# Attention and recurrence of a hybrid trunk layer: each store issued by the engine that makes its data

## The chip, the cores and the metric

The kernel runs on one core of a Trainium2 chip. The metric is the time of one execution on the device in microseconds (us); of several runs the median is given. The core has TensorE (PE in the profile, with its weight loads as PEld), VectorE (DVE), ScalarE (ACT), GpSimd (POOL) and SyncE (SP). Each works through its own instructions in order. A DMA is issued by an instruction in the queue of one engine, and an engine whose next instruction has to wait holds back everything behind it.

## The reference, cut to what matters

One layer of a hybrid backbone on 1024 latent tokens and 256 prompt tokens, 1024 channels, in float32. The normalised input is projected to everything that the two mixers need. Attention has 8 heads of 64 on 2 key/value heads; latent tokens read 512 cached and 1024 latent keys, prompt tokens read the 256 prompt keys. The recurrence (HGRN) has 4 heads of 128 and runs forwards and backwards in chunks of 32.

```python
z = h @ w_in
hq, hf_f, hf_b, hi, hg, aq, ak, av, gl = jnp.split(z, _split_points(), axis=-1)
...
s = jnp.einsum('bqkgd,bskd->bkgqs', qi, kf) * scale
p = jax.nn.softmax(s, axis=-1)
return jnp.einsum('bkgqs,bskd->bqkgd', p, vf)
...
def step(s, inp):
    dec, kv_n = inp
    return dec[..., None] * s + kv_n, s
...
merged = g[:, :, 0] * (o_h @ w_ho) + g[:, :, 1] * (o_a @ w_ao)
return merged @ w_out, k, v, s_final
```

Behind it come a gated residual, a second norm, a squared-ReLU MLP and the last norm. Outputs are both token sets, the prompt's new keys and values, and the final states of the recurrence.

## The kernel before, in words

All products are made in three passes of split operands (a rounded high part and the rest). The order of TensorE's instructions is the order in which the program is written (L50); the instructions of the other engines are put in order by a scheduler from its own estimate of when each can run, SyncE's DMA issues among them, up to the MLP (from L1332 SyncE's order is the written one too). Tiles come from rings of a few buffers (L31 to L43): a tile is written again only when the readers of its former content are done. Query loads, key loads, scratch of the recurrence and the exponentials' high parts share ring X with 20 buffers; weight loads (`wraw`, L293) have two buffers, their split forms (`wsp`, L298) six.

**Attention** (`attention`, L804) is made of 20 units: 16 of one head by 512 latent queries with 12 key blocks of 128, and 4 of two heads by 256 prompt queries with 2 key blocks. Keys lie on the partitions, so a score tile is 128 keys by 512 queries. A unit does this:
- `load_q` (L691) loads its queries from scratch in DRAM as Ql (Qp for the prompt), `load_q2` (L695) once more as Q2, whose row 64 is kept for the maxima.
- `top` (L700) makes a first score (L708) whose maximum over the keys (L709) is wanted for each query. `top_row` (L713) turns the four columns of maxima into rows (`mrow`) and four small DMAs, one for each block of 128 queries, put them into row 64 of Q2, so that the next product subtracts them.
- `score` (L722) makes the score tile of one key block (L726) in one of two PSUM banks; ScalarE takes the exponential in place in PSUM (L728) and copies its rounded high part out as pTh (L730), VectorE makes the rest, pTl (L731), GpSimd adds up pTh (pacc, L735).
- `value` (L738) multiplies with the values (L745, L746); `sums` (L753) adds the row sums (L755); `scale` (L766) divides on GpSimd (oa, L771) and stores the result to DRAM (OA).

These steps of neighbouring units overlap by a table of due times in units of one score step (L815 to L833): the queries of a unit are loaded 15 steps before its first score and first used 1.9 steps later; the row of maxima of the unit before it is due 0.4 steps ahead of that load; the result of the unit before that is stored 6 steps after its last score.

Between the steps of attention TensorE works on the **projections for the recurrence** (`Filler`, L364): `z_ch` (L343) makes channels by tokens, `z_tok` (L323) tokens by channels. Each result is taken out of PSUM by a function `..._consume` and stored to DRAM: queries QD by ScalarE alone (`hq_consume`, L849), forget gates FD by ScalarE and then VectorE (`hf_consume`, L857), values VD by ScalarE (`hi_consume`, L867), output gates GD by ScalarE, VectorE and then GpSimd (`hg_consume`, L874). All these evacuation tiles (`ze`) come from one ring of four.

The **recurrence** (`hgrn`, L1043) has 24 units (head, direction, token tile). Each loads uf, uq, uv and, backwards, ug from that scratch (`prep`, L895), runs scans on VectorE, and is filled up on TensorE with the projection of the branch gates (`gl_consume`, L1086, stored as GT). The transposed result is taken out by ScalarE and stored as OH (`out_t`, L1034); the final states come from VectorE and are stored to the output (L1067).

In the kernel before all of these stores are issued by SyncE with the helper `dma` (L106), in the same queue as the loads of queries, keys, values, scratch and weights. The helper `store` (L109), which issues from GpSimd's queue, serves the small rows of sums, the gate rows, and the MLP.

Of the kernel before, what the change touches and what calls it, by code (L numbers as in the profile page):

```python
# [15 lines left out]
P = 128  # L16
# [29 lines left out]
def build(ctx, tc, I, O, C):  # L46
    nc = tc.nc
    v, s_, g_, pe, sp = nc.vector, nc.scalar, nc.gpsimd, nc.tensor, nc.sync
# [8 lines left out]
    def pool(name, side="left"):  # L57

        st = open_pools[name] = ExitStack()
        return st.enter_context(tc.tile_pool(name=name, bufs=1, side=side, reuse_waits="tile"))  # L60
# [16 lines left out]
    def PS(tag, shape=(P, 512)):  # L77
        if tag in turn and not rings_of_two:
            turn[tag] += 1
            tag = third[tag] if turn[tag] % 3 == 0 else tag  # L80
        return ps.tile(list(shape), F32, tag=tag, name="ps_" + tag, bufs=PSB[tag])

    def S(shape=(P, 512), dt=F32, name=None, ring=None):
        ring = ring or RING_OF[name]
        return (xb if ring == "X" else sb if ring in "DE" else sl).tile(list(shape), dt, tag="s" + ring, name=name, bufs=RINGS[ring])

    def res(store, t, kc, name):

        if t < 2:
            store[t][kc] = S(name=name)  # L90
        elif kc % 2 == 0:
            x = S((P, 2, 256), name=name)
            store[t][kc], store[t][kc + 1] = x[:, 0, :], x[:, 1, :]
        return store[t][kc]
# [8 lines left out]
    def DR(shape, name, dt=F32):  # L103
        return dp.tile(list(shape), dt, name=name)

    def dma(out, in_):  # L106
        sp.dma_start(out=f32(out), in_=f32(in_))

    def store(out, in_):  # L109
        g_.dma_start(out=f32(out), in_=f32(in_))  # L110

    def f32(ap):
        return ap.bitcast(F32)
# [486 lines left out]
    for idx in range(len(steps)):  # L600
        while idx >= KC - 1 and done <= min(idx + AHEAD, len(steps) - 1):
            t, kc = steps[done]
# [7 lines left out]
        t, kc = steps[idx]  # L610
# [59 lines left out]
    OH = [[DR((P, n), "OH%d_%d" % (c, t)) for t, (_, n, _) in enumerate(TT)] for c in range(4)]  # L670

    class Unit:
# [40 lines left out]
        def top_row(self):  # L713

            pt = PS("t")
            pe.transpose(pt[0:4, 0:P], self.ngm, ident)
            r = S((4, P), F32R, name="mrow")
            s_.activation(r, pt[0:4, 0:P], AF.Copy)
            for b in range(4):
                dma(self.q2[64:65, b * P:(b + 1) * P], r[b:b + 1, :])  # L720

        def score(self, k):  # L722
            kg, b = self.kt[k]
# [29 lines left out]
        def sums(self):  # L753

            pe.matmul(self.pl, sel1[0], self.acc, start=False, stop=True, skip_group_check=True)  # L755
            r = S(name="prow")
            with tc.high_priority(offset=400):
                s_.activation(r[64:65], self.pl[64:65], AF.Copy)
                v.tensor_tensor(self.o, self.pl[0:64], self.o, op=ALU.add)
            row, inv, rs = SR[self.h][self.t], RR[self.h][self.t], T(4, "rs")  # L760
            store(row, r[64:65])
            g_.dma_start(out=rs, in_=row.rearrange("o (p j) -> (o p) j", j=4))
            v.reciprocal(rs, rs)
            store(inv.rearrange("o (p j) -> (o p) j", j=4), rs)

        def scale(self):  # L766

            row = RR[self.h][self.t]
            o, rb = self.o, S((64, 512), name="prb")
            g_.dma_start(out=rb, in_=row.broadcast_to([64, 512]))  # L770
            g_.tensor_tensor(o, o, rb, op=ALU.mult)  # L771
            oa = OA[self.h // 2][self.t]
            if self.t < 2:
                d0 = (self.h % 2) * 64
                dma(oa[d0:d0 + 64, :], o)
            else:
                dma(oa.rearrange("(h d) n -> d h n", h=2), self.view(o))

    SR = [[DR((1, 512), "SR%d_%d" % (h, t)) for t in range(3)] for h in range(8)]
    RR = [[DR((1, 512), "RR%d_%d" % (h, t)) for t in range(3)] for h in range(8)]  # L780
# [63 lines left out]
    QD = [[DR((P, n), "QD%d_%d" % (h, t)) for t, (_, n, _) in enumerate(TT)] for h in range(4)]  # L844
    FD = [[[DR((P, n), "FD%d_%d_%d" % (d, h, t)) for t, (_, n, _) in enumerate(TT)] for h in range(4)] for d in range(2)]
    VD = [[DR((P, NB[t], 256), "VD%d_%d" % (c, t)) for t in range(3)] for c in range(2)]
    GD = [[DR((P, NB[t], 256), "GD%d_%d" % (c, t)) for t in range(3)] for c in range(2)]

    def hq_consume(c):  # L849
        def f(half, t, po):  # L850
            n = TT[t][1]
            e = S(name="ze")
            s_.activation(e[:, 0:n], po, AF.Copy, scale=float(P) ** -0.5)
            dma(QD[2 * c + half][t], e[:, 0:n])
        return f

    def hf_consume(d, c):  # L857
        def f(half, t, po):
            n = TT[t][1]
            h = 2 * c + half  # L860
            e = S(name="ze")
            s_.activation(e[:, 0:n], po, AF.Tanh, scale=0.5)
            v.tensor_scalar(e[:, 0:n], e[:, 0:n], fc1[:, d, h:h + 1], fc0[:, d, h:h + 1], op0=ALU.mult, op1=ALU.add)
            dma(FD[d][h][t], e[:, 0:n])
        return f

    def hi_consume(c):  # L867
        def f(pr, po):
            e = S((P, 2, 256), name="ze")
            s_.activation(e, po, AF.Copy)  # L870
            dma(VD[c][pr // 2][:, 2 * (pr % 2):2 * (pr % 2) + 2], e)
        return f

    def hg_consume(c):  # L874
        def f(pr, po):
            e = S((P, 4, P), name="ze")
            po4 = po.rearrange("p b (h d) -> p (b h) d", h=2)
            s_.activation(e, po4, AF.Tanh, scale=0.5)
            v.scalar_tensor_tensor(e.rearrange("p a d -> p (a d)"), e.rearrange("p a d -> p (a d)"), 1.0,
                                   po.rearrange("p b d -> p (b d)"), op0=ALU.add, op1=ALU.mult)  # L880
            g_.tensor_tensor(e, e, hnb.unsqueeze(1).broadcast_to([P, 4, P]), op=ALU.mult)
            dma(GD[c][pr // 2][:, 2 * (pr % 2):2 * (pr % 2) + 2], e.rearrange("p (b h) d -> p b (h d)", b=2))
        return f


    class HUnit:
# [147 lines left out]
        def out_t(self):  # L1034
            nb = self.nb
            pt = PS("t", (P, 4, P))
            for b in range(nb):
                pe.transpose(pt[:, b, :], self.o[:, b], ident)
            e = S((P, 4, P), name="oT")
            s_.activation(e[:, 0:nb], pt[:, 0:nb], AF.Copy)  # L1040
            dma(OH[self.h][self.t], e[:, 0:nb].rearrange("p b d -> p (b d)"))

    def hgrn(fill):  # L1043

        units = hunits
        fwd = {u.h: {} for u in units}
        for u in units:
            u.fwd = fwd[u.h].get(u.t)
            fwd[u.h][u.t] = u
        N, LATE = len(units), 3  # L1050

        share = [u.n + 128.0 for u in units] + [300.0] * LATE
        tot, done, st = sum(share), 0.0, None
        units[0].keys_t()
        for i in range(N + LATE):
            part = lambda x: fill.to((done + x * share[i]) / tot)
            if i + 1 < N:
                units[i + 1].prep()
            if i < N:
                u = units[i]  # L1060
                part(0.25)
                u.scores(u.fwd)
                part(0.5)
                u.states_(u.st or st)
                st = u.last
                if u.t == 2:
                    dma(O["new_state_hgrn"][u.d, u.h], st)  # L1067
                part(0.75)
            if i >= LATE and units[i - LATE].d == 1:
                units[i - LATE].out_t()  # L1070
            if 1 <= i <= N:
                units[i - 1].out(units[i - 1].fwd)
            part(0.95)
            if i + 1 < N:
                units[i + 1].keys_t()
            if 1 <= i <= N and units[i - 1].d == 1:
                units[i - 1].gate(units[i + 1] if i + 1 < N else None)
            part(1.0)
            done += share[i]


    GT = [[DR((P, n), "GT%d_%d" % (c, t)) for t, (_, n, _) in enumerate(TT)] for c in range(16)]

    def gl_consume(c):
        def f(half, t, po):
            n = TT[t][1]  # L1086
            e = S(name="ze")
            s_.activation(e[:, 0:n], po, AF.Tanh, scale=0.5)
            dma(GT[2 * c + half][t], e[:, 0:n])
        return f  # L1090

    def zh(c):
# [65 lines left out]
    for t in MT:  # L1158
        n = TT[t][1]
        for c in range(8):  # L1160
            r = S(name="or")
# [18 lines left out]
    for c2 in range(4):  # L1180
        r = wp.tile([P, 8, 256], F32, tag="wraw", name="wraw", bufs=2)
        for i, nm in enumerate(("w_hgrn_out", "w_attn_out")):
            dma(r[:, 4 * i:4 * i + 4, :], I[nm][:, c2 * 256:(c2 + 1) * 256].rearrange("(k p) c -> p k c", p=P))
        for half in range(2):
# [4 lines left out]
            for t in MT:  # L1189
                n = TT[t][1]  # L1190
# [108 lines left out]
    for b, half in turns:  # L1299
        t, off = b // 4, (b % 4) * P  # L1300
# [62 lines left out]
    def raw1(i):  # L1363
        return wraw(I["w_ff1"], KC, i * 256)
# [30 lines left out]
    for i in range(NP):  # L1395
        r = raw1(i)
        for half in range(2):
# [6 lines left out]
            if half == 0:  # L1404

                x = pw.tile([P, 4, P], F32, tag="at", name="at", bufs=4)
                e = pw.tile([P, 4, P], F32, tag="ap", name="ap", bufs=3)
# [124 lines left out]
    st = pool("st")  # L1532
# [291 lines left out]
```

## Time and profile before

| | |
|---|---|
| median of 3 runs | 2151.84 us (2149.25 to 2152.53) |
| the profiled execution | 2148.34 us |
| its span in the profile | 2146.6 us |
| mean granted clock of TensorE | 0.983 of full speed |
| VectorE busy | 1358.9 us (63%) |
| ScalarE busy | 967.0 us (45%) |
| GpSimd busy | 670.4 us (31%) |
| DMA: queue of SyncE (hardware) | 281.92 MB, 41.0% of 16 engines' span |
| DMA: queue of GpSimd (software) | 42.41 MB, 5.8% |

All times in the profile are counted from the start of the span, in us unless marked ns. A line of the waits reads: engine, what it was about to make, its line, `<-` whom it waited for, then the total, how many times, and the longest. A line of the timeline reads: start, duration, engine, line, operation, out`<-`in, count, and in brackets the idle time just before it with what ended it. SPq is SyncE's queue of DMA issues; since every such issue goes through one helper, they all have its line, L107, and are told apart by tile names. The time of a DMA issue is the time it takes on the issuing engine; the time to landing is the transfer's own. In names of tiles the buffer numbers are left out, so Q2 stands as `Q`. Attention runs from about 190 to 790 us, the recurrence from there to about 1090, the output projection to about 1300, then the MLP.

### The profile page before, as it was taken

What the parts mean: (1) busy time and instruction counts of PE and PEld (TensorE: products, weight loads), DVE (VectorE), ACT (ScalarE), POOL (GpSimd) and SP (SyncE); (2) the same over time, 40 slices, a digit from 0 to 9 for tenths busy, and PEclk for the clock granted to TensorE, in tenths of its full rate; (3) what the DMA queues carried; (4) which work ended last, traced back from release to release, by engine and by line L of the source; (5) the groups of instructions that cost most, each with busy time, mean ns of one, the idle gap of its engine ahead of it and who ended that gap; (6) DMA issues with size and microseconds to landing.
All of it is one profiled execution on the core that took longest, in us unless ns stands there. A gap on an engine that the chain in (4) does not pass through costs nothing.

```text
span 2146.6 us, 31802 instructions
## 1 busy us (share of the span) xinstructions
PE 2025.3 (94%) x11296; PEld 1697.0 (79%) x11296; DVE 1358.9 (63%) x2405; ACT 967.0 (45%) x1812; POOL 670.4 (31%) x757
## 2 busy tenths in 40 slices
PE   6899988988989978999999999999999999999997
PEld 4698767876767867888888888998888888888886
DVE  4785654555655556987644644866666666667785
ACT  4764655555555622222240323764454544333442
POOL 1461455564545654655402200121222210000010
PEclk9999999999999988999999999999999999999999
DMA  9365223133222233554564442584444459545773
GB/s 298 124 202 158 64 82 89 42 107 106 73 79 69 77 123 114 160 169 133 179 198 135 136 157 106 185 260 146 157 143 157 160 213 373 190 146 177 229 255 112
DMA packets 242496, 326.36 MB, mean 152 GB/s; under 512 B 27640, under 2 KB 158800, under 8 KB 242336
## 3 DMA queue, kind: packets, MB, share of 16 engines
q1 hardware_dynamic: 227040, 281.92, 41.0%
q0 software_dynamic: 15296, 42.41, 5.8%
q8 instruction: 89, 1.46, 0.3%
q14 instruction: 71, 0.58, 0.1%
HBM read 236.55 MB, written 87.65 MB: 151 GB/s over the span
## 4 chain that ended last, share of the span: by engine, by line
PE 56%; DVE 4%; DMA 2%; ACT 1%; issue 1%; POOL 0%; SPq 0%; DVEq 0%; POOLq 0%; ACTq 0%
PE ps_g L319 3%; PE ps_g L321 3%; PE ps_g L320 3%; PE ps_v L319 2%; PE ps_g L1627 1%; PE ps_v L321 1%; PE ps_v L320 1%; PE ps_g L1625 1%; PE ps_g L1626 1%; PE ps_t L1625 1%; PE ps_t L1626 1%; PE ps_t L1627 1%; PE ps_s L1475 1%; PE ps_t L1473 1%; PE ps_t L1474 1%; PE ps_t L1475 1%
## 5 line engine op out<-in xcount | busy, mean ns | idle before, releaser
L319 PE MATMUL ps_g<-hs,wsp 128*128 128x512 f32 (+1 forms) x688 | 250.4, 364 | 0.0
L735 POOL TENSOR_TENSOR pacc<-pacc,pTh 128x512 f32<-128x512 f32 x160 | 208.4, 1303 | 117.8 <-ACT pTh L730 102.8
L321 PE MATMUL ps_g<-hs,wsp 128*128 128x512 f32 (+1 forms) x688 | 241.7, 351 | 1.4 <-DVE wsp L291 1.4
L320 PE MATMUL ps_g<-hs,wsp 128*128 128x512 f32 (+1 forms) x688 | 241.8, 352 | 0.0
L290 ACT ACTIVATE wsp<-wraw 128x1024 fp32r<-128x1024 f32 x110 | 109.7, 998 | 264.6 <-PE ps_g L320 73.7
L291 DVE TENSOR_TENSOR wsp<-wraw,wsp 128x1024 fp32r<-128x1024 f32 x110 | 135.4, 1232 | 138.5 <-ACT wsp L290 138.2
L731 DVE TENSOR_TENSOR pTl<-ps_s,pTh 128x512 fp32r<-128x512 f32 x200 | 137.3, 687 | 114.0 <-ACT pTh L730 97.4
L728 ACT ACTIVATE ps_s<-ps_s 128x512 f32<-128x512 f32 x200 | 116.6, 583 | 198.5 <-PE ps_s L726 180.2
L709 DVE TENSOR_REDUCE mx<-ps_t 128x1 f32<-128x512 f32 (+1 forms) x208 | 136.7, 665 | 83.8 <-PE ps_t L708 82.9
L290 ACT ACTIVATE ah<-ar 128x640 fp32r<-128x640 f32 (+1 forms) x112 | 81.0, 723 | 190.7 <-PE ps_v L1626 102.3
L319 PEld LDWEIGHTS ps_g<-hs,wsp 128*128 128x128 f32 x688 | 131.8, 192 | 23.7 <-issue 5.0
L321 PEld LDWEIGHTS ps_g<-hs,wsp 128*128 128x128 f32 x688 | 131.3, 191 | 19.6 <-DVE wsp L291 1.6
L320 PEld LDWEIGHTS ps_g<-hs,wsp 128*128 128x128 f32 x688 | 132.0, 192 | 17.6 <-issue 0.2
L291 DVE TENSOR_TENSOR ah<-ar,ah 128x640 fp32r<-128x640 f32 (+1 forms) x112 | 89.8, 802 | 80.3 <-ACT ah L290 79.9
L708 PE MATMUL ps_t<-Kl,Ql 128*128 128x512 f32 x192 | 85.0, 443 | 46.7 <-DMA Ql<-QS 38.2
L730 ACT ACTIVATE pTh<-ps_s 128x512 fp32r<-128x512 f32 x200 | 119.4, 598 | 13.5 <-ACT ps_s L728 0.4
L172 POOL TENSOR_TENSOR frst<-ms,mexp 128x1 f32<-128x1 f32 x10 | 11.4, 1152 | 362.7 <-DVE ssf L1714 278.4
L336 PE MATMUL ps_g<-wsp,hs 128*128 128x256 f32 x400 | 117.6, 294 | 0.0
L338 PE MATMUL ps_g<-wsp,hs 128*128 128x256 f32 x400 | 114.5, 286 | 0.0
L337 PE MATMUL ps_g<-wsp,hs 128*128 128x256 f32 x400 | 114.4, 286 | 0.0
L708 PEld LDWEIGHTS ps_t<-Kl,Ql 128*128 128x128 f32 x192 | 37.1, 193 | 63.2 <-DMA Ql<-QS 42.5
L336 PEld LDWEIGHTS ps_g<-wsp,hs 128*128 128x128 f32 x400 | 77.7, 194 | 10.4 <-issue 2.4
(562 smaller groups left out, 5914.7 us busy)
## 6 DMA issues: line engine op xcount, KB each, us to landing
ar<-AF SPq DMA_DIRECT2D x112, 320.0 KB, 3.3
wraw<-in_w_ff SPq DMA_DIRECT2D x32, 1024.0 KB, 5.8
wr<-in_w_ff SPq DMA_DIRECT2D x128, 256.0 KB, 4.3
wraw<-in_w_in SPq DMA_DIRECT2D x18, 1024.0 KB, 6.3
wraw<-in_w_ada SPq DMA_DIRECT2D x16, 1024.0 KB, 6.0
AF<-a POOLq DMA_DIRECT2D x48, 256.0 KB, 2.7
AF<-t POOLq DMA_DIRECT2D x48, 256.0 KB, 2.5
wa<-in_w_ada SPq DMA_DIRECT2D x32, 256.0 KB, 5.9
```

What stands on the lines that cost most here:

```text
L290: s_.activation(hi, raw, AF.Copy)
L291: v.tensor_tensor(lo, raw, f32(hi), op=ALU.subtract)
L319: pe.matmul(out, hi[:, k, :], mh, start=(first and k == 0), stop=False)
L320: pe.matmul(out, hi[:, k, :], ml, start=False, stop=False)
L321: pe.matmul(out, lo[:, k, :], mh, start=False, stop=(last and k == kcs - 1))
L336: pe.matmul(po[:, bb, :], mh[:, off:off + P], wh[:, k % 4, :], start=(k == 0), stop=False)
L708: pe.matmul(pq[:, 0:n], self.q1[:, b * P:(b + 1) * P], K[self.g][0][self.kts[i]], start=True, stop=True)
L709: v.tensor_reduce(self.mx[:, i:i + 1], pq[:, 0:n], axis=AX.X, op=ALU.max)
L728: s_.activation(pq, pq, AF.Exp)
L730: s_.activation(hi, pq, AF.Copy)
L731: v.tensor_tensor(lo, pq, f32(hi), op=ALU.subtract)
L735: g_.tensor_tensor(self.acc, f32(self.pt[0][0]) if k == 1 else self.acc, f32(hi), op=ALU.add)
```

## The change

A helper `store_act` issues a DMA from ScalarE's queue. Ten stores in nine functions leave SyncE (the one of OA in two forms). To ScalarE go those whose data ScalarE makes: the row of maxima (80 issues), QD (12), VD (10), OH (12) and GT (48). To GpSimd, by the helper `store`, go OA (20 issues) and GD (10), whose data GpSimd makes, and FD (24) and the final states (8), whose data VectorE makes, which issues no DMA. What is stored, from where and to where, and all tiles, rings and due times are the same. The loads all stay on SyncE; so do the stores of the stage before attention (keys, queries and values to scratch).

```diff
     def store(out, in_):
         g_.dma_start(out=f32(out), in_=f32(in_))
+
+    def store_act(out, in_):
+
+        s_.dma_start(out=f32(out), in_=f32(in_))
...
             r = S((4, P), F32R, name="mrow")
             s_.activation(r, pt[0:4, 0:P], AF.Copy)
             for b in range(4):
-                dma(self.q2[64:65, b * P:(b + 1) * P], r[b:b + 1, :])
+                store_act(self.q2[64:65, b * P:(b + 1) * P], r[b:b + 1, :])
...
             if self.t < 2:
                 d0 = (self.h % 2) * 64
-                dma(oa[d0:d0 + 64, :], o)
+                store(oa[d0:d0 + 64, :], o)
             else:
-                dma(oa.rearrange("(h d) n -> d h n", h=2), self.view(o))
+                store(oa.rearrange("(h d) n -> d h n", h=2), self.view(o))
...
-            dma(QD[2 * c + half][t], e[:, 0:n])
+            store_act(QD[2 * c + half][t], e[:, 0:n])
...
-            dma(FD[d][h][t], e[:, 0:n])
+            store(FD[d][h][t], e[:, 0:n])
...
-            dma(VD[c][pr // 2][:, 2 * (pr % 2):2 * (pr % 2) + 2], e)
+            store_act(VD[c][pr // 2][:, 2 * (pr % 2):2 * (pr % 2) + 2], e)
...
-            dma(GD[c][pr // 2][:, 2 * (pr % 2):2 * (pr % 2) + 2], e.rearrange("p (b h) d -> p b (h d)", b=2))
+            store(GD[c][pr // 2][:, 2 * (pr % 2):2 * (pr % 2) + 2], e.rearrange("p (b h) d -> p b (h d)", b=2))
...
-            dma(OH[self.h][self.t], e[:, 0:nb].rearrange("p b d -> p (b d)"))
+            store_act(OH[self.h][self.t], e[:, 0:nb].rearrange("p b d -> p (b d)"))
...
                 if u.t == 2:
-                    dma(O["new_state_hgrn"][u.d, u.h], st)
+                    store(O["new_state_hgrn"][u.d, u.h], st)
...
-            dma(GT[2 * c + half][t], e[:, 0:n])
+            store_act(GT[2 * c + half][t], e[:, 0:n])
```

## The prediction

> **What bounds the kernel now.** I read the page first, then the waits of TensorE, then the waits of SyncE's DMA queue, then the two engines' timelines side by side where TensorE stands still.
>
> ```profile
> span 2146.6 us, 31802 instructions
> PE 2025.3 (94%) x11296; PEld 1697.0 (79%) x11296; DVE 1358.9 (63%) x2405; ACT 967.0 (45%) x1812; POOL 670.4 (31%) x757
> ```
>
> The span is 2146.6 us; TensorE is busy for 2025.3 of it. What can be won is in the 121 us in which TensorE is idle, and in stretches in which it works at a lower clock. The windows say where the edited stages stand:
>
> ```profile
> 190.00:490.00 300.00, 268.38 (x1438) 221.81 (x1438) 171.10 (x304) 162.25 (x289) 153.50 (x140) 0.96 0.28 84
> 490.00:790.00 300.00, 270.86 (x1502) 222.71 (x1502) 173.59 (x299) 162.60 (x290) 166.07 (x156) 0.97 0.26 76
> 850.00:1090.00 240.00, 237.79 (x1870) 200.71 (x1870) 179.82 (x422) 67.20 (x183) 115.41 (x132) 0.99 0.52 162
> ```
>
> The columns are the stretch and its length, then the busy time of TensorE, its weight loads, VectorE, ScalarE and GpSimd, then the granted clock. In attention (190 to 790) TensorE is idle for 31.6 + 29.1 = 60.7 us; in the recurrence (850 to 1090) for 2.2. So attention decides. Who makes TensorE wait there:
>
> ```profile
> PE ps_t L708 <- DMA Ql<-QS: 38.2, 13, 5.6
> PE ps_t L966 <- DVE usf L937: 16.9, 2, 14.8
> PE ps_t L708 <- DVE mx L709: 8.5, 11, 1.3
> PE ps_t L708 <- DMA Qp<-QS: 7.6, 4, 3.7
> PE ps_s L726 <- DVE pTl L731: 6.8, 2, 6.1
> ```
>
> Three quarters of attention's idle time, 38.2 + 7.6 = 45.8 us in 17 gaps, is the first product with a freshly loaded query block (Ql, or Qp for the prompt) waiting for that load. The load is short once it is issued:
>
> ```profile
> DMA to landing us min/median/max: 3.2/3.5/8.2
> ```
>
> So why is it issued late? Around the gap that ends at 299.27, SyncE's queue and then TensorE:
>
> ```profile
> 284.21 8.04 SPq L107 DMA_DIRECT2D OA<-oa  x2
> 292.34 2.45 SPq L107 DMA_DIRECT2D Q<-mrow  x4
> 294.89 0.53 SPq L107 DMA_DIRECT2D FD<-ze  x1
> 295.52 0.38 SPq L107 DMA_DIRECT2D Ql<-QS  x1
> ```
> ```profile
> 299.27 0.80 PE L708 MATMUL ps_t<-Kl,Ql 128*128 128x512 f32 x1 [5.12 <-DMA Ql<-QS]
> ```
>
> TensorE wanted Ql at 299.27 - 5.12 = 294.15. SyncE works its queue in order, and from 284.21 to 295.52 it had nothing but stores: two OA stores (the second waited for GpSimd), four issues for the row of maxima, one FD store. Over the whole kernel these waits are
>
> ```profile
> SPq L107 <- DVE wsp L291: 354.1, 38, 27.0
> ...
> SPq L107 <- POOL oa L771: 105.8, 18, 13.4
> SPq L107 <- DVE ze L863: 92.1, 13, 17.0
> ```
>
> The top row is no store: weight loads (wraw) wait there for their buffer. The bound, then, is TensorE, and in attention a load behind stores in one queue.
>
> **The change, part by part.** The sum is made against the profiled execution, 2148.34 us (span 2146.6 and 1.7 around it). The median shown is 2151.84, 3.5 more; I add that at the end.
>
> *The query loads.* All stores ahead of Ql and Qp (mrow to ScalarE, OA, FD and GD to GpSimd, VD and QD to ScalarE) leave the queue. In the gap above the load could have gone out at 284.7, 9.4 us ahead of need, against the 0.4 + 3.5 that it takes. So most of the 45.8 us goes. What is late next in the queue is the weight load, which stays on SyncE. In four of the 17 gaps one stands close ahead of the load; the first of them:
>
> ```profile
> 366.63 0.39 SPq L107 DMA_DIRECT2D wraw<-in_w_ada  x1
> 367.12 0.53 SPq L107 DMA_DIRECT2D Ql<-QS  x1
> ```
> ```profile
> 373.78 0.50 PE L708 MATMUL ps_t<-Kl,Ql 128*128 128x512 f32 x1 [3.44 <-DMA Ql<-QS]
> ...
> 526.10 0.50 PE L708 MATMUL ps_t<-Kl,Ql 128*128 128x512 f32 x1 [2.44 <-DMA Ql<-QS]
> ...
> 596.04 0.79 PE L708 MATMUL ps_t<-Kl,Ql 128*128 128x512 f32 x1 [5.59 <-DMA Ql<-QS]
> ...
> 664.21 0.50 PE L708 MATMUL ps_t<-Kl,Qp 128*128 128x256 f32 x1 [3.75 <-DMA Qp<-QS]
> ```
>
> These four are 3.44 + 2.44 + 5.59 + 3.75 = 15.2 us. At 366.63 the weight load itself waited for its buffer; in the others stores stood ahead as well. I keep half, 8 us (between 0 and 15.2). Term: -45.8 + 8 = -37.8.
>
> *What the gaps cost behind them.* After a long gap TensorE gets half its clock:
>
> ```profile
> 300.00:302.00 2.00, 2.00 (x9) 1.71 (x7) 0.69 (x1) 0.41 (x1) 0.00 (x0) 0.50 0.00 0
> ```
>
> Over attention the clocks 0.96 and 0.97 are worth 0.04 x 300 + 0.03 x 300 = 21 us. Part of that falls into idle time, which is counted already, and part follows the 6.1 us wait on pTl, which stays; I estimate that 13 of the 21 come back. Term: -13 (between 0 and -17). The Trainium skill, "TensorE: Matmul & The Clock Gate", section "Part 1: The HAM clock gate", puts the fall to half clock after an idle window of about 3.4 us; the trace agrees for the 5.12 us gap, and by that rule alone only the gaps above 3.4 us would give anything back, some 1.7 us each.
>
> *ScalarE's new work.* There is no DMA issue on ScalarE in the profile before. The nearest rows are SyncE's issues of the same stores, and one of GpSimd's of a row of 2 KB:
>
> ```profile
> L107 SPq DMA_DIRECT2D Q<-mrow x80: 497/582/1323, 192.7 to 732.0; - x80
> L107 SPq DMA_DIRECT2D GT<-ze x48: 319/320/2193, 795.4 to 1123.0; - x48
> ```
> ```profile
> L110 POOL DMA_DIRECT2D SR<-prow x20: 510/529/584, 236.9 to 780.7; - x20
> ```
>
> I take SyncE's medians: it is the same transfer. A unit of attention (20 of them) then has a burst of 4 x 0.582 = 2.33 us on ScalarE, behind which the exponentials queue. How much delay do these stand? The scores run through two PSUM banks, so score k + 2 needs pTl of score k:
>
> ```profile
> 460.16 0.48 PE L726 MATMUL ps_s<-Ql,Kl 128*128 128x512 f32 x1
> ...
> 463.19 0.39 PE L726 MATMUL ps_s<-Ql,Kl 128*128 128x512 f32 x1
> ```
> ```profile
> 456.89 0.69 DVE L731 TENSOR_TENSOR pTl<-ps_s,pTh 128x512 fp32r<-128x512 f32 x1 [0.37 <-ACT pTh L730]
> 460.86 0.67 DVE L731 TENSOR_TENSOR pTl<-ps_s,pTh 128x512 fp32r<-128x512 f32 x1
> ```
>
> pTl of one score is done at 456.89 + 0.69 = 457.58 and the score two on starts at 460.16: 2.58 us to spare; for the next, 461.53 and 463.19: 1.66. Mean 2.1, so a burst costs about 2.33 - 2.1 = 0.2 us; some scores have less to spare, so I take 0.3 each, +6 us. Below nothing is excluded, since ScalarE only gets work. Above, at the longest issue of that row: (4 x 1.323 - 1.66) x 20 = 73. The other stores on ScalarE (10 VD and 12 QD in attention, 12 OH and 48 GT mostly in the recurrence, at about 0.32 us) follow their own activation at once and are single: nothing. In the recurrence ScalarE is busy for 67.2 of 240 us, and that is their cover; gone, 60 x 0.32 = 19 us.
>
> *GpSimd's new work.* 20 OA, 24 FD, 10 GD and 8 states, at the 0.53 us of the SR row: 33 us, on an engine busy for 319.6 of attention's 600. Those for OA and GD wait for GpSimd's own result; FD waits for VectorE, and behind it on GpSimd stand the running sums of the exponentials, wanted by the product at L755. SyncE's wait for FD averaged 92.1 / 13 = 7.1 us, and it came to the store with nothing else to do, so GpSimd's will be shorter. The row sum is wanted 4.3 score steps after the last score. A step is
>
> ```profile
> L726 PE MATMUL ps_s<-Ql,Kl x192: 388/393/794, 196.9 to 769.1; 128*128 128x512 f32 x192
> ```
>
> (769.1 - 196.9) / 199 = 2.88 us (200 scores with the prompt's 8), so 12.4 us. That covers it: nothing. If the cover went, 13 waits that exceed it by (17.0 - 12.4) at the longest cost up to 60 us, but the longest is one.
>
> *What stays.* The 14.8 us wait for usf stands between attention and recurrence, and follows a weight load:
>
> ```profile
> 785.41 8.09 DMA wraw<-in_w_in
> ```
>
> VectorE has the split of these weights in front of its scans in its order, so earlier uf loads do not help. The 8.5 us on mx are VectorE's and the 6.1 on pTl come from VectorE doing the first unit's scans: both stay. Stages behind 1140 issue none of the moved stores.
>
> Sum: 2148.3 - 37.8 - 13 + 6 = 2103.5 us; on the scale of the median, 2107.
>
> A rule speaks against this size. The Trainium skill, "DMA: Bandwidth & Descriptors", section "Issuing engines are not separate DMA queues", says that issuing from several engines saves only the sequencer's time to issue. By that rule each of the 17 gaps loses at most the 2.33 us of its four issues, 39.6 us in place of 45.8, and the sum would be 2113. The row of 105.8 us of waiting for oa speaks against it: a queue in order also loses the time for which its head waits.
>
> **The rivals.**
>
> 1. *Only issue time is saved* (for it: the query load's buffer may come free only shortly before SyncE came to it; against it: the wait list around that gap has no entry but oa). 45.8 becomes 39.6: 2148.3 - 39.6 + 8 - 13 + 6 + 3.5 = 2113. Chance 0.10.
> 2. *Weight loads take the stores' place.* SyncE's waits for wsp are the largest, 354.1 us over 38 waits; if the new order puts such a load ahead of the query load in half of the units, half of the gaps (23 us) and of the clock (6.5) stays: 2148.3 - 22.8 - 6.5 + 6 + 3.5 = 2128. Chance 0.13.
> 3. *The query load was bound by its buffer all along*, so that it is issued as late as before; the 45.8 us merely change the name of what they wait for: 2152 with the bursts hidden, 2158 with them. Against it speaks the same wait list. Chance 0.08.
> 4. *Slower: ScalarE becomes what the scores wait for.* One mechanism: four issues in a row before each unit, each holding the exponentials. At the row's longest, 1.323 us an issue, (5.29 - 2.1) x 20 = 64 us are lost against 51 won: 2148.3 + 13 + 3.5 = 2165. It decides from 4t - 2.1 = 51 / 20 = 2.55, that is t = 1.16 us an issue. For it: no row shows an issue on ScalarE, and these four have a wait each; against it: SyncE's median is half of that. Chance 0.11.
>
> **How the numbers follow.** The forecast as summed has the remaining 0.58: 2107 us. Its own range is 2085 (no gap left, 17 of clock, no bursts, some of mx) to 2125. The range of all reaches to rival 2 with bursts of twice the size: 2085 to 2140, which leaves out rivals 3 and 4, 0.19. A measurement tells about 0.2% (4.3 us) from no change. Faster: 0.58 + 0.10 + 0.13 = 0.81; within: 0.05 of rival 3; slower: the rest of it and rival 4, 0.14.
>
> **What would show it.** Right: TensorE's waits for Ql and Qp together under 12 us; no wait of SyncE for oa, ze or mrow; attention's clock at 0.99; issues of mrow on ScalarE near 0.58 us; the last product at L755 some 45 us earlier than 779; TensorE's wait for pTl under 15. Wrong: Ql waits as long as before (rival 3), or behind wraw (rival 2); waits for pTl of 50 us and more, or issues on ScalarE above 1.1 us (rival 4); long waits on GpSimd for ze with L755 waiting for pacc.

## The result and the profile after

The changed kernel takes 2162.46 us (median of 4 runs, 2162.20 to 2163.19) against 2150.55 us for the kernel before (4 runs, 2146.79 to 2152.53). The ratio is 1.0058 with a 95% interval of 1.0041 to 1.0075: slower by about 0.6%. The forecast was 2107, with 2085 to 2140 as its range; it was wrong in sign. One execution, of f1 below, took 2527.55 us at a granted clock of 0.749; it stands in no median and no ratio here.

The changed kernel's profiled execution took 2162.41 us, 14.1 more than the one before (2148.34). Below, lines behind the new helper are four higher than before: L712 is the old L708, L730 the old L726, L735 the old L731, and the issues on ScalarE stand as `ACTq L114`.

First the head of its page, then the windows of attention (in two halves) and recurrence. The columns are those of the prediction's windows.

```profile
span 2160.5 us, 31742 instructions
...
PE 2029.0 (94%) x11296; PEld 1697.2 (79%) x11296; DVE 1366.1 (63%) x2405; ACT 962.6 (45%) x1812; POOL 704.7 (33%) x819
```
```profile
190.00:490.00 300.00, 273.23 (x1476) 224.65 (x1475) 177.71 (x315) 163.87 (x298) 169.91 (x167) 0.97 0.28 85
490.00:790.00 300.00, 261.39 (x1372) 213.72 (x1372) 170.87 (x288) 153.75 (x279) 172.72 (x173) 0.94 0.23 69
850.00:1090.00 240.00, 233.06 (x1888) 195.63 (x1888) 180.07 (x424) 65.98 (x178) 121.31 (x143) 1.00 0.50 156
```

The span is 13.9 us longer. Of these, 3.1 come ahead of the first score, which starts at 200.0 instead of 196.9; the first moved store is already 3.2 us late (159.9 instead of 156.8), and over all the runs below the first score starts anywhere from 196.9 to 204.0, not in step with their times. So I put these 3.1 us down to none of the edits. From the first score to the last product at L755 (now L759) attention takes 592.3 us instead of 582.3, which is most of the loss. GpSimd has 34 us more work, as forecast. The first half of attention has become a little better (273.2 us of TensorE's work done in it instead of 268.4), the second half worse (261.4 instead of 270.9, at a clock of 0.94 instead of 0.97). In the recurrence TensorE is idle for 6.9 us instead of 2.2. What TensorE waits for:

```profile
PE ps_s L730 <- DVE pTl L735: 29.1, 20, 8.0
PE ps_t L970 <- DVE usf L941: 20.3, 4, 15.1
PE ps_t L712 <- DMA Ql<-QS: 19.3, 5, 7.9
...
PE ps_t L712 <- DMA Qp<-QS: 8.9, 2, 6.0
PE ps_t L712 <- DVE mx L713: 8.4, 11, 1.2
...
PE ps_w L759 <- POOL pacc L739: 1.0, 1, 1.0
```

Two rows tell most of the story. The wait for the query load (Ql and Qp) fell from 45.8 us in 17 gaps to 19.3 + 8.9 = 28.2 us in 7: fewer gaps, but longer ones. And the wait for pTl, the low half of the exponentials, rose from 6.8 us in 2 waits to 29.1 us in 20. Adding up all gaps of TensorE over the span gives 109.3 us before and 122.9 after, 13.6 more, which is nearly the longer span. (TensorE's busy time, 3.7 us more, and the stretch behind its last product, 3.3 us less, about cancel.)

**The query load.** SyncE's waits, the three stores of before gone from the top, show what took their place:

```profile
SPq L107 <- DVE wsp L295: 450.6, 42, 36.5
...
SPq L107 <- PE ps_v L749: 178.8, 29, 16.3
...
SPq L107 <- DMA Q<-mrow: 30.9, 5, 9.7
```

The wait for wsp, which weight loads have ahead of them, rose from 354.1 to 450.6 us. The place of the longest gap, on SyncE and then on TensorE:

```profile
431.23 0.38 SPq L107 DMA_DIRECT2D wraw<-in_w_ada  x1
431.71 0.78 SPq L107 DMA_DIRECT2D wraw<-in_w_in  x1
432.58 1.04 SPq L107 DMA_DIRECT2D Ql<-QS  x1
```
```profile
440.94 0.76 PE L712 MATMUL ps_t<-Kl,Ql 128*128 128x512 f32 x1 [7.89 <-DMA Ql<-QS]
```

TensorE wanted the load at 440.94 - 7.89 = 433.05. SyncE stood 9.0 us at the first weight load, waiting for VectorE's split of earlier weights (wsp); then it issued two weight loads of 1 MB each, and the query load behind them. The load landed 8.2 us after its issue, where the median of before was 3.5. So a weight load ahead costs twice: its wait, and the bytes that it puts ahead. I counted the rows that stand directly ahead of the 18 query loads that attention issues: a weight load stands there 8 times (twice with the prompt's query load, issued 0.6 us earlier, in between), before 2 times. Six of the seven gaps stand behind one, all but a gap of 3.01 us.

**The exponentials.** ScalarE around the row of maxima of one unit, and TensorE's next score:

```profile
355.44 0.27 ACT L722 ACTIVATE mrow<-ps_t 4x128 fp32r<-4x128 f32 x1 [0.37 <-PE ps_t L720]
355.74 2.50 ACTq L114 DMA_DIRECT2D Q<-mrow  x4
358.34 1.07 ACT L732 ACTIVATE ps_s<-ps_s 128x512 f32<-128x512 f32 x2 [2.63 <-issue]
359.43 1.06 ACT L294 ACTIVATE wsp<-wraw 128x1024 fp32r<-128x1024 f32 x1
360.40 1.07 ACT L734 ACTIVATE pTh<-ps_s 128x512 fp32r<-128x512 f32 x2
```
```profile
362.40 0.50 PE L730 MATMUL ps_s<-Ql,Kl 128*128 128x512 f32 x1 [2.18 <-DVE pTl L735]
```

The four issues hold ScalarE for 2.50 us. Behind them its order has two exponentials in a row, then a split of weights, and only then the copies to pTh on which pTl waits. In the kernel before an exponential is followed by its own copy nearly always: over attention I count 2 places where two exponentials come first, and 21 in the changed kernel, nearly all just behind a burst. So the burst delays pTl by its own length and, through the order behind it, by one more exponential (about 0.58 us) or more. Of the 20 waits for pTl, 15 stand within 11 us of a burst's start and add up to 18.9 us. They are far from equal: the last unit alone has 4.8 us behind its burst and 8.0 at its end, where the kernel before has 6.1.

### The profile page after: what moved, and what is told of

The parts are those of the page before. It is cut to its first block, busy times and chain, and to the rows that moved or that the text cites. A ratio compares the mean times of both kernels' runs of the same rounds, so it can differ in the third digit from the quotient of the medians.

```text
span 2160.5 us, 31742 instructions
## 1 busy us (share of the span) xinstructions
PE 2029.0 (94%) x11296; PEld 1697.2 (79%) x11296; DVE 1366.1 (63%) x2405; ACT 962.6 (45%) x1812; POOL 704.7 (33%) x819
## 4 chain that ended last, share of the span: by engine, by line
PE 55%; DVE 5%; DMA 1%; issue 1%; ACT 1%; POOL 1%; DVEq 0%; POOLq 0%; ACTq 0%; SPq 0%
PE ps_g L323 3%; PE ps_g L324 3%; PE ps_g L325 3%; PE ps_g L1631 1%; PE ps_g L1629 1%; PE ps_g L1630 1%; PE ps_t L1629 1%; PE ps_t L1631 1%; PE ps_t L1630 1%; PE ps_v L323 1%; PE ps_t L1478 1%; PE ps_t L1477 1%; PE ps_t L1479 1%; PE ps_v L325 1%; PE ps_v L324 1%; PE ps_s L1629 1%
## 5 line engine op out<-in xcount | busy, mean ns | idle before, releaser
L295 DVE TENSOR_TENSOR wsp<-wraw,wsp 128x1024 fp32r<-128x1024 f32 x110 | 140.6, 1279 | 163.3 <-ACT wsp L294 157.7
L735 DVE TENSOR_TENSOR pTl<-ps_s,pTh 128x512 fp32r<-128x512 f32 x200 | 136.1, 686 | 109.8 <-ACT pTh L734 87.1
L324 PEld LDWEIGHTS ps_g<-hs,wsp 128*128 128x128 f32 x688 | 131.6, 191 | 17.6 <-issue 0.2
L712 PE MATMUL ps_t<-Kl,Ql 128*128 128x512 f32 x192 | 84.1, 439 | 27.7 <-DMA Ql<-QS 19.3
L730 PE MATMUL ps_s<-Ql,Kl 128*128 128x512 f32 x192 | 81.0, 422 | 26.8 <-DVE pTl L735 26.8
```

The lines of the kernel that those rows point to most:

```text
L295: v.tensor_tensor(lo, raw, f32(hi), op=ALU.subtract)
L324: pe.matmul(out, hi[:, k, :], ml, start=False, stop=False)
L735: v.tensor_tensor(lo, pq, f32(hi), op=ALU.subtract)
```

## The experiments

Theory A: the loss is made by the bursts of four issues on ScalarE, and the expected gain is not made because a query load now stands behind weight loads on SyncE. Theory B: every edit makes the scheduler order the other engines anew, and the time is that of another order, whatever is moved. Theory C: the loss is made in the recurrence, whose stores (OH, GT, states) moved too. All diffs below are against the changed kernel or the one before, as said; line numbers in their profiles are those of before (L708, L726, L731), with the issues on ScalarE as L115. "Ql wait" is TensorE's wait for Ql and Qp together.

| kernel | median us | ratio to before | Ql wait | pTl wait | pairs of exponentials |
|---|---|---|---|---|---|
| before | 2150.55 | 1 | 45.8 | 6.8 | 2 |
| the change | 2162.46 | 1.0058 (1.0041 to 1.0075) | 28.2 | 29.1 | 21 |
| e1_no_mrow | 2146.68 | 0.9995 (0.9977 to 1.0013) | 33.3 | 12.7 | 2 |
| e2_mrow_only | 2153.82 | 1.0017 (0.9998 to 1.0036) | 28.5 | 24.3 | 18 |
| e3_ql_act | 2118.14 | 0.9850 (0.9830 to 0.9869) | 14.7 | 7.4 | 2 |
| e4_att_only | 2163.98 | 1.0059 (1.0040 to 1.0078) | 26.8 | 34.6 | 21 |
| f1_chg_mrow_pool | 2140.39 | 0.9948 (0.9929 to 0.9966) | 6.4 | 11.9 | 2 |
| f2_chg_early | 2143.25 | 0.9960 (0.9939 to 0.9981) | 0 | 39.2 | 19 |
| f3_chg_ql_act | 2170.59 | 1.0083 (1.0059 to 1.0108) | 44.4 | 16.6 | 20 |
| f4_ql_act_early | 2112.30 | 0.9817 (0.9798 to 0.9835) | 0 | 15.9 | 5 |
| g1_early | 2121.50 | 0.9872 (0.9851 to 0.9893) | 0 | 16.9 | 5 |
| g2_chg_two_act | 2139.77 | 0.9951 (0.9929 to 0.9974) | 20.7 | 13.7 | 4 |
| g3_nomrow_ql_act_early | 2110.85 | 0.9827 (0.9804 to 0.9850) | 0 | 13.4 | 5 |
| g4_chg_mrow_pool_early | 2139.75 | 0.9948 (0.9931 to 0.9966) | 0 | 12.4 | 3 |

Ratios are to the kernel before as it ran on the same chip beside each (its medians there were 2149.53, 2151.55 and 2150.89 for the e, f and g runs).

### e1: the change without the row of maxima

```diff
-                store_act(self.q2[64:65, b * P:(b + 1) * P], r[b:b + 1, :])
+                dma(self.q2[64:65, b * P:(b + 1) * P], r[b:b + 1, :])
```

> The change, but the four stores of the row of maxima stay on SyncE. Theory A (bursts of four issues on ScalarE hold the exponentials, and weight loads hold the query loads on SyncE): TensorE's wait for pTl falls from 29.1 us to 10 or less, its wait for Ql and Qp stays between 15 and 35, time 2135 to 2150. Theory B (the scheduler's other order of the compute engines costs the time, wherever the row is issued): pTl wait stays at 20 or more, time 2155 to 2165. Theory C (the loss is made in the recurrence): time as the change, 2160.

The other nine stores moved, by themselves, do nothing that can be measured. Against the whole change 0.6%, some 14 us, come back, and the two intervals do not touch: with the nine others moved, the row of maxima on ScalarE is what makes the change slower. TensorE's waits and SyncE's:

```profile
PE ps_t L708 <- DMA Ql<-QS: 26.4, 12, 3.7
...
PE ps_s L726 <- DVE pTl L731: 12.7, 5, 8.0
```
```profile
SPq L107 <- DVE wsp L291: 413.1, 42, 36.1
...
SPq L107 <- ACT mrow L718: 155.3, 18, 27.0
```

With the burst back on SyncE the pTl wait is down to 12.7. Theory A had 10 or less: 5.9 us more than the 6.8 of before are there without any burst on ScalarE, most of them in the last unit (waits of 2.9 and 8.0 us). And the query load is still waited for, in 16 short gaps: SyncE, free of the other stores, now runs ahead and stands at mrow, whose data is not there yet. One gap, on SyncE and TensorE:

```profile
574.05 2.43 SPq L107 DMA_DIRECT2D Q<-mrow  x4
576.58 0.51 SPq L107 DMA_DIRECT2D Ql<-QS  x1
```
```profile
580.69 0.79 PE L708 MATMUL ps_t<-Kl,Ql 128*128 128x512 f32 x1 [3.72 <-DMA Ql<-QS]
```

The due times explain part of it. The row of maxima is due 0.4 steps ahead of the load and the load is first used 1.9 steps later, 1.9 x 2.88 = 5.5 us. Behind the four issues it needs 2.4 + 3.5 = 5.9 us (the 3.5 count from the start of its own issue). In the same queue as the row it is late without any other store. This sum gives 0.4 us, and the 16 gaps are 2.1 us on average; how late the row's data was in each is not worked out here.

### e2: only the row of maxima on ScalarE

The one line of e1, the other way round, in the kernel before.

> The kernel before, with only the four stores of the row of maxima on ScalarE. Theory A: wait for pTl 20 to 30 us; wait for Ql and Qp falls from 45.8 to 30 to 40, since OA still stands ahead; time 2150 to 2165, not faster than before. Theory B: pTl wait may be anything, time within 5 us of before. Theory C: no loss, time 2130 to 2145.

```profile
PE ps_t L708 <- DMA Ql<-QS: 24.4, 9, 6.9
PE ps_s L726 <- DVE pTl L731: 24.3, 16, 6.1
```

With the 4.1 us for Qp, this one edit makes both halves of the picture: 17.3 us of Ql wait gone, 17.5 us of pTl wait come. (30 to 40 us of Ql wait had been expected to stay; it is 28.5.) The time is that of before within its interval. With the stores of OA and FD still on SyncE, 3 of 18 query loads stand directly behind a weight load, 4 more with one other issue or two in between. So the 0.6% is no sum of its parts: the row alone costs 0.17%, which cannot be told from nothing, the nine others alone nothing (e1). What the two do to each other no run here takes apart.

### e3: the query load on ScalarE's queue, nothing else

```diff
     def load_q(self):
-            dma(self.view(self.q1), self.q_of(P))
+            store_act(self.view(self.q1), self.q_of(P))
```

> The kernel before, all stores on SyncE, with only the 20 query loads Ql and Qp moved to ScalarE's queue. Theory A (the load is late because of what stands ahead of it in SyncE's queue): wait for Ql and Qp under 10 us, half-clock stretches mostly gone, pTl wait up by 5 at most: time 2095 to 2120. Rival (its buffer comes free late): the wait stays at 30 to 45 us, and ScalarE, which now waits for the buffer, holds the exponentials: time 2155 to 2180.

```profile
PE ps_t L708 <- DMA Ql<-QS: 10.9, 11, 2.4
...
PE ps_s L726 <- DVE pTl L731: 7.4, 2, 6.9
...
PE ps_t L708 <- DMA Qp<-QS: 3.8, 2, 3.6
```

All stores stay on SyncE, only the load leaves, and the kernel is 1.5% faster than before. From issue to landing it takes as long as before (median 3.4 us, 3.5 before), so the transfer is not what got better; nor can its buffer have been what it waited for. That is the diagnosis on which the prediction rested: the load was late for its place in the queue. The wait left, 14.7 us, is above the 10 expected; f4 below removes it. One issue of 0.33 us does not hurt the exponentials (pTl 7.4 against 6.8).

### e4: the change without the recurrence's stores

OH, GT and the states stay on SyncE; all else as in the change.

> The change without its recurrence part: OH, GT and the final states stay on SyncE. Theory A: attention as in the change, TensorE's idle time from 830 to 1100 falls from 7 us to about 2: time 2155 to 2160. Theory C: the loss goes, time 2150 or less. Theory B: another order again, no forecast within 10 us.

```profile
PE ps_s L726 <- DVE pTl L731: 34.6, 19, 13.6
```

In the recurrence (850 to 1120) TensorE's idle time is back from 6.9 us to 2.5 (2.2 before); the time is not better, and a little above the 2155 to 2160 expected. So that stage has a part of about 4.5 us in the change, but theory C does not carry the loss. All kernels divide in this way: where OH, GT and the states are moved (eight kernels) this idle time is 5.3 to 7.0 us, where they stay on SyncE (six) 2.0 to 2.5.

### f1: the change with the row of maxima on GpSimd

```diff
-                store_act(self.q2[64:65, b * P:(b + 1) * P], r[b:b + 1, :])
+                store(self.q2[64:65, b * P:(b + 1) * P], r[b:b + 1, :])
```

> The change, but the row of maxima goes to GpSimd's queue in place of ScalarE's, so no store of it is on SyncE or ScalarE. Theory A: wait for pTl 5 to 13 us (29.1 in the change), wait for Ql and Qp stays near 28, because weight loads hold them: time 2135 to 2148. Theory B (reordering by the scheduler): pTl wait stays above 20, time 2155 or more. Rival: GpSimd's bursts of 2.2 us hold the running sums, and TensorE waits for pacc by 10 us or more.

```profile
PE ps_s L726 <- DVE pTl L731: 11.9, 6, 6.2
PE ps_s L726 <- DMA Q<-mrow: 11.5, 4, 3.8
...
PE ps_w L755 <- POOL pacc L735: 7.0, 2, 4.1
```

ScalarE is rid of the burst, and pTl with it; the Ql wait is nearly gone as well, with 4 of 18 loads behind a weight load. That was not expected: it was to stay near 28 us, behind the weight loads. Which engine issues the row thus changes the order on SyncE too. But a part of the price moves: GpSimd issues behind its running sums, so the row comes late (11.5 us where there were 0.2) and the sums too (7.0).

### f2: the change, with the query load two steps earlier

```diff
-            ev += [(-15.0, u.load_q, ()), (-6.9, u.load_q2, ()), (-3.4, u.top_row, ())]
+            ev += [(-17.0, u.load_q, ()), (-6.9, u.load_q2, ()), (-3.4, u.top_row, ())]
```

> The change, with the query load due 17 score steps ahead of its unit in place of 15, so that it comes ahead of more weight loads in SyncE's order. Theory A: wait for Ql and Qp falls from 28 to 15 or less, pTl wait stays at 22 to 35: time 2135 to 2150. Rival (the buffer of the load comes free late): the wait stays at 25 or more, time 2155 to 2165.

```profile
PE ps_s L726 <- DVE pTl L731: 39.2, 19, 8.0
```

No wait for a query load is left, and 1.0% against the change comes back, some 21 us. The pTl wait grows to 39.2 us: with four issues on ScalarE it is there with and without the Ql gaps (22 to 35 had been expected).

### f3: the change with the query load on ScalarE too

> The change, and the 20 query loads also on ScalarE's queue. Theory A, with the two losses adding: wait for Ql and Qp under 15 us, pTl wait 22 to 38 us; time 2128 to 2145, that is between 10 and 27 us over the kernel before with the query loads alone moved (2118). If the loads alone decided: 2118 or less.

This expectation was missed, and the miss is instructive. ScalarE, with the burst and the load behind it, SyncE at that time, and TensorE:

```profile
437.26 2.69 ACTq L115 DMA_DIRECT2D Q<-mrow  x4
...
440.13 0.45 ACTq L115 DMA_DIRECT2D Ql<-QS  x1
```
```profile
439.12 0.38 SPq L107 DMA_DIRECT2D wraw<-in_w_ada  x1
439.61 0.65 SPq L107 DMA_DIRECT2D wraw<-in_w_in  x1
```
```profile
447.42 0.77 PE L708 MATMUL ps_t<-Kl,Ql 128*128 128x512 f32 x1 [6.47 <-DMA Ql<-QS]
```

The same edit that won 1.5% in e3 makes the change slower still. What the load has to get away from is the row of maxima due just ahead of it; here both moved, and it stands behind the burst again, in another queue: 14 of the 18 loads come directly behind one. In the gap shown the 2.69 us of the burst let two weight loads of 1 MB go out on SyncE first, and the load took 7.2 us to land. So another queue does not spare it the bytes that are under way. The Ql wait is 44.4 us, as before.

### f4, g1, g3: the load early, without the burst on ScalarE

f4 is the kernel before with the edits of e3 and f2; g1 the kernel before with the one number of f2 alone; g3 the change without the row of maxima (e1), with both edits.

> The kernel before with only the query loads on ScalarE, due 17 steps ahead in place of 15. Theory A: the 14.7 us of wait that were left come from the load being written only 1.9 steps ahead of its use, so the wait falls under 3 us, time 2098 to 2112. Rival (buffer free late): ScalarE waits for buffers, pTl wait over 15, time 2118 or more.

> The kernel before, all stores on SyncE, with only the query load due 17 score steps ahead in place of 15, so that it is written ahead of the row of maxima of its neighbour and not behind it. Theory A: the four issues and ScalarE's wait no longer stand ahead of it, OA and ze still do: wait for Ql and Qp 10 to 25 us (45.8 before), pTl under 12: time 2118 to 2138. If the two steps alone are enough, as the row of 17 gaps of at most 5.6 us would allow: under 5 us, 2105 to 2118.

> All moved stores but the row of maxima as in the change (that row stays on SyncE), and the query loads on ScalarE, due 17 steps ahead. Theory A: wait for Ql and Qp near 0, pTl 8 to 18. If the other stores cost or give nothing once the query load has left their queue: time within 6 us of the 2112 of the same loads with all stores on SyncE. If a free SyncE queue still helps: 2105 or less. If the stores on GpSimd and ScalarE cost: 2118 or more.

In all three the Ql wait is zero; g1, the one number, is 1.3% faster than before, f4 1.8% and g3 1.7%. For g1 a wait of 10 to 25 us had been expected, because OA and the other stores stay ahead; the two steps were enough for these as well. Its pTl wait, 16.9, is above the 12 expected. TensorE's waits in f4, without the one at the change of stages:

```profile
PE ps_s L726 <- DVE pTl L731: 15.9, 8, 7.8
PE ps_t L708 <- DVE mx L709: 12.8, 16, 1.7
...
PE ps_s L726 <- DMA Q<-mrow: 4.5, 3, 2.4
```

g3 moves nine stores that f4 leaves on SyncE, and the two cannot be told apart (2110.85 and 2112.30): once the load is free, moving these stores gains nothing over the whole kernel. In one profile each, though, attention from its first score to the last product at L755 takes 538.1 us in g3 and 544.9 in f4 (577.4 in e1, 582.3 before), and in the recurrence TensorE is idle for 5.3 us in g3 and 2.0 in f4. The stores of attention may thus gain what those of the recurrence lose; no run here moves the former alone. g3 and f4 are the fastest kernels of the study; f4 ends 0.3 us above its range, g3 within.

### g2, g4: the dose of the burst

g2 is the change with two of the four issues on ScalarE and two on GpSimd; g4 is f1 with the early load of f2.

```diff
-                store_act(self.q2[64:65, b * P:(b + 1) * P], r[b:b + 1, :])
+                (store_act if b < 2 else store)(self.q2[64:65, b * P:(b + 1) * P], r[b:b + 1, :])
```

> The change with the row of maxima shared out: two of the four issues on ScalarE, two on GpSimd. Theory A (the longer the burst on ScalarE, the longer the wait for pTl): pTl wait between the 11.9 us of none and the 29.1 of four, 14 to 24; time between 2142 and 2162, 2145 to 2158.

> The change with the row of maxima on GpSimd and the query load due 17 steps ahead. Theory A: wait for Ql and Qp under 3 us, pTl 10 to 20, and what stays is TensorE's wait for the row itself and for pacc, 10 to 20 us: time 2122 to 2140, still over the 2112 of the kernel before with the loads moved.

With two issues the pTl wait is 13.7 us and the pairs of exponentials are 4; with none it is 11.9 in f1. So half the burst costs next to nothing and the whole one 15 us and more: that looks like a threshold, and not like a price per issue. The expectation (14 to 24 us, 2145 to 2158) had a price per issue, and missed. In g4 the Ql wait is zero, but the row on GpSimd comes late, by more than expected (with pacc 24.0 us, 10 to 20 expected):

```profile
PE ps_s L726 <- DMA Q<-mrow: 20.5, 8, 6.2
```

**What follows together.** All five kernels with four issues in a row on ScalarE have 18 to 21 pairs of exponentials; the other nine have 2 to 5. The pTl wait is 24 to 39 us in four of the five (in f3 it is 16.6, with 44.4 us of gaps for the load beside it) and 7 to 17 in the nine. That is theory A for the loss, and theory B as a part of it: the longer wait comes by the burst and by the order planned around it, and no run here parts these two. As a cause by itself B does not fit: e1 orders nine stores anew and the time stays; g1 changes one number, and of the 29.4 us that it wins 20.9 are fewer gaps of TensorE (109.3 to 88.4) and 7.7 less half clock. For the gain that was not made, the four kernels that have all of attention's stores off SyncE, and the load there at its old due time, stand in order: 8 of 18 loads behind a weight load and 28.2 us of Ql wait in the change, 8 and 26.8 in e4, 6 and 20.7 in g2, 4 and 6.4 in f1. Differences of a few microseconds between two orders I leave unexplained.

## Why the prediction was wrong

The sum for the profiled execution was 2103.5 us, and 2162.4 was measured: 58.9 off. By terms:

| term | forecast | measured | off by |
|---|---|---|---|
| waits for Ql and Qp | -37.8 | 28.2 - 45.8 = -17.6 | +20.2 |
| half clock behind gaps, while TensorE works | -13 | 19.8 - 19.3 = +0.5 | +13.5 |
| bursts on ScalarE (wait for pTl) | +6 | 29.1 - 6.8 = +22.3 | +16.3 |
| all other gaps | 0 | 13.6 + 17.6 - 22.3 = +8.9 | +8.9 |

The measured terms are differences of the two traces; the clock term is the share of full speed missing, summed over the busy part of each microsecond from 190 to 850. They add up to 58.9.

- **The diagnosis was right.** "In attention a load behind stores in one queue": e3, g1 and f4 take the load out of its place and win 1.3% to 1.8%. The third rival (its buffer) is out. ("The 0.4 + 3.5 that it takes" counts the issue twice, since the row of 3.5 us starts with it; nothing hangs on that.)
- **The first step that failed** is "All stores ahead of Ql and Qp [...] leave the queue. [...] So most of the 45.8 us goes", with 8 us kept for the weight loads. What stands ahead of the load was read from the old order; the new order filled the place. The weight loads, which the prediction named as the next late thing, stand directly ahead of 8 loads out of 18, and not in "four of the 17 gaps": the second rival, given 0.13, which kept 23 us of the wait where 28.2 were measured. How the scheduler would fill the place was not worked out, and the runs show only that it did, differently with each edit (8, 6, 4 loads).
- **The clock term** hung on that step. It was right for what it supposed: where the gaps do go, the loss of 19.3 us falls to 11.6 (g1), 7.1 (f4) and 6.5 (g3), which is the forecast's -13 at most. In the change the seven gaps left are mostly long ones (the clock fell at six of them). Behind the gap of 7.89 us:

```profile
444.00:446.00 2.00, 2.00 (x6) 1.55 (x5) 1.28 (x2) 0.00 (x0) 1.28 (x1) 0.50 0.00 0
446.00:448.00 2.00, 2.00 (x8) 1.57 (x8) 0.56 (x1) 0.71 (x2) 0.00 (x0) 0.76 0.00 0
```

TensorE worked at half clock until past 446.

- **The second step that failed** is "a burst costs about 2.33 - 2.1 = 0.2 us; [...] I take 0.3 each, +6 us". The price of an issue was right:

```profile
L114 ACTq DMA_DIRECT2D Q<-mrow x80: 504/601/1190, 195.9 to 736.2; - x80
```

0.601 us against 0.582. What was wrong is the slack: 2.1 us is what a score has to spare when its own exponential and copy come at once, and behind the burst they do not. With one more exponential ahead of the copy an estimate of the cost is 2.50 + 0.58 - 2.1 = 1.0 us in each of 20 units. Measured were 22.3 / 20 = 1.1 against the kernel before, and 16.4 / 20 = 0.8 against e1, which has the other moves without the burst; the units differ (0.3 to 4.8 us in 15 of them), and the slack of 2.1 comes from two scores, so the agreement is partly luck. The fourth rival named this mechanism, and came close in its time (2165) by luck: its condition, 1.16 us an issue, was not met, the issue was half as long and the slack was used up by others, and it counted 51 us as won of which 17 were.
- **The other gaps.** GpSimd's term was right: its wait for FD's data (ze) is 20.2 us over 13 waits, and the row sums were late once, by 1.0 us. (One more wait, of 32.6 us, stands ahead of the first FD store at 194.9, before the first score.) In the recurrence the idle time went from 2.2 to 6.9 us between 850 and 1120 where nothing was forecast; e4 shows it to come with OH, GT and the states. Another 2.0 us of gaps stand ahead of 190; the rest is small and open. What was to stay stayed: mx 8.4 us, and the wait for usf at the change of stages 15.1.
- **The rule that spoke against the size.** By the Trainium skill, "DMA: Bandwidth & Descriptors", section "Issuing engines are not separate DMA queues", another issuing engine saves only the time to issue. e3 shows more: 20 issues of 0.33 us moved to another queue, and 31.1 us of waiting and 1.5% of the time gone, since the load no longer waits for what waits ahead of it. The measurement decides against this rule for a load behind waiting instructions. In e1, where nine other stores moved and the load stayed behind the row of maxima, nothing measurable was won.

## What to carry to other kernels

If a load is late because of its queue, move the load (or its due time), not what happens to stand ahead of it: another order finds something else to put there, and here one changed number (g1) won 1.3% where ten moved stores lost 0.6%. Before DMA issues are given to an engine that feeds the critical loop, compare the whole burst, plus the work queued behind it, with the slack of that loop: two issues of 0.6 us cost next to nothing here, four in a row did not. And read the gain of a change that touches several stages stage by stage: e1 comes out even although TensorE's idle time in the recurrence is 4 us longer in it.

## What was not expected of the hardware

- Loads on SyncE waited for stores of ScalarE to complete (`DMA Q<-mrow`, 30.9 us in 5 waits, the longest 9.7, in the changed kernel). One of them, of 8.2 us, stands ahead of a weight load, which touches neither the row nor Q2. Three others, 5.2 to 9.7 us, stand ahead of query loads, for none of which TensorE had to wait. In f1 and g2, where less or nothing of the row is stored by ScalarE, the trace has no such wait; the cause wasn't tried.
- An issue in ScalarE's queue took 0.33 us for a query load of 256 KB (e3) and 0.60 us for a quarter row of maxima; on SyncE before the medians are 0.53 and 0.58, and on GpSimd the quarter row took 0.49 us (f1).
- In the changed kernel a query load issued directly behind weight loads of 1 MB landed 5.2 to 8.2 us after its issue, the others 2.9 to 3.4 us (10 of the 18 loads, whose landing the trace tells). In f3, where load and weights were issued by two engines, it was 7.2 us.
- Half clock needs no single long gap: in the changed kernel it came behind two gaps of 2.88 and 1.56 us with 0.7 us of products between them (granted clock 0.50 from 669 to 672), and behind one of 3.01 us. In the kernel before, a gap of 3.00 us that ends at 409.30 had it from 408.3 to 415.1, and one of 2.90 us that ends at 559.76 left the clock at 1.00.
